# S5 mixer of a four-layer diffusion backbone: the two turned-back products are added before the output product, the outputs follow one block later, and the tables' transfers change buffers and order

## The chip, the cores and the metric

The kernel runs on one core of a Trainium2 chip. The metric is the device time of one execution in microseconds, the median of several runs. TensorE (PE), VectorE (DVE), ScalarE (ACT) and GpSimd (POOL) work beside each other, each in the order of its own instruction queue; SyncE's queue (SP) issues most of the transfers, and GpSimd's queue the rest.

## The reference

Four layers run over 256 latent tokens and 256 context tokens of width 1024. Layer 1 mixes tokens with a bidirectional diagonal state-space layer (S5) and a gated output; the other layers pool or attend, and each layer ends with a gated ConvFFN.

```
for direction in range(2):                       # forwards, and backwards in time
    a_bar, b_bar = discretise(a_re, a_im, log_dt, b_re, b_im)
    h_ctx = scan(a_bar, einsum('blgc,gpc->blgp', u_ctx, b_bar), reverse)
    h0 = h_ctx[:, 0] if reverse else h_ctx[:, -1]     # the context's last state enters the latent scan
    bu = einsum('blgc,gpc->blgp', u_lat, b_bar); bu[entry] += a_bar * h0
    h_lat = scan(a_bar, bu, reverse)
    y += real(einsum('blgp,gcp->blgc', h, c))
g = gelu(y + d_skip * u)
out = (g @ w1 + b1) * sigmoid(g @ w2 + b2)
```

There are 64 groups of 16 channels, each with 64 complex states.

## The kernel before, in words

The mixer (`s5_mixer`) handles the 64 groups in 8 blocks of 8 groups, both token streams at once. Eight tokens form a chunk, so that a scan runs over chunks only; what happens inside a chunk is held in tables. Four kinds of tables are computed during the FFN of layer 0 (`s5_tables`), written to DRAM, and loaded again, 1 MB each: `b` (per block: tokens to states), `c` (per block: states to tokens), `k` (per two blocks: token to token inside a chunk), `r` (per two blocks: cosines and sines by which states are turned, so that the scan has real decay factors).

One block m takes these steps:

- `finish_u` (L1473 and after): two operations that finish the normalised input tile U, on VectorE for blocks 0 and 1, on GpSimd for the others;
- `v_mm`: TensorE multiplies U by `b` into two PSUM tiles v, one per direction;
- `turned` and `decay`: ScalarE writes the sines with both signs into a part of the tile `us` (`signs`, two sets, used in turn) and the decay factors into `rtab`;
- `scan`: VectorE turns v (two products and a sum per direction: L1521, L1524, L1526) and scans it into the tile g (L1528). Then the states are turned back: GpSimd forms y1 = g times cosine (L1532) and y2 = g with real and imaginary part exchanged times sine (L1533). In block 7 y2 is formed on VectorE;
- `z_mm`: TensorE adds into the PSUM tile z the products of U with `k` (16 records of this kind in the trace per block) and of y1 and then of y2 with `c` (64 records each), and ScalarE applies the GELU (tile G).

`back` and `back_in` send G through DRAM, two blocks at a time, to change its layout, on GpSimd's queue; `split_hi` and `split_lo` split it into a high and a low part (gh, gl) for the GLU (`glu_mm`), whose weights come in 1 MB blocks (raw), are split by ScalarE (whi) and VectorE (wlo, L159), and are multiplied three times (hi·hi, hi·lo, lo·hi). Beside the GLU run the modulation chunks of a later step (ada): ScalarE scales, VectorE and GpSimd add up (ads, L321).

Order and buffers: every engine takes its instructions as the program writes them. The loop over m in `s5_mixer` runs scan(m), U of m + 4, signs and decay of m + 2, v of m + 2, then z of m. The table `S5HOME` says for each table load in which buffer it lands: x0 to x2 are three buffers of their own (they exist only once the tables are computed), and raw, whi, wlo and ada are the weights' buffers, two each, shared in turn. A load waits until the buffer's former content has been read. `s5_ahead` runs during the last steps of the FFN of layer 0, once per 128 channels; after every second one it writes the inputs of two blocks out (s5dU) and issues some table loads and the loads of U, in a layout by groups. The loads into x0 to x2 stand at the end of `s5_tables`. In the mixer, the table `ready` ties each further load to a step of a block. All of them go through SP's one queue.

Of the kernel before, what the change touches and what calls it, by code (L numbers as in the profile page):

```python
# [9 lines left out]
F32 = mybir.dt.float32  # L10
# [6 lines left out]
P = 128  # L17
# [15 lines left out]
S5HOME = dict(t.split(":") for t in (  # L33
    "r0:x0 k0:x1 b1:x2 b0:ada c0:ada b2:whi c1:wlo b3:whi c2:wlo r2:raw k2:raw b4:ada b5:whi c3:ada r4:x0 b6:whi "
    "c4:wlo k4:x1 b7:ada c5:wlo k6:x2 r6:raw c6:ada c7:wlo").split())
GLU = ((0, 0), (1, 0), (0, 1), (1, 1), (2, 0), (2, 1), (3, 0), (3, 1))
# [8 lines left out]
class Net:  # L45
# [1209 lines left out]
    def s5_tables(self):  # L1255
# [147 lines left out]
    def s5_ahead(self, d):  # L1403
# [31 lines left out]
        self.s5_loads(("U4", "U6") if d == 7 else todo)  # L1435

# [4 lines left out]
    def s5_mixer(self, l):  # L1441
# [70 lines left out]
        def scan(m):  # L1512
# [17 lines left out]

            y1, y2 = (y[:, 1:1025].rearrange("p (d c n) -> p d c n", d=2, c=2) for y in ys[m % 2])
            nc.gpsimd.tensor_mul(y1, g, cs)  # L1532
            (V if m == KD - 1 else nc.gpsimd).tensor_mul(y2, g[:, :, ::-1], sn[:, :, ::-1])  # L1533

        G = {}

        def z_mm(m):
            ct, kt = (self.s5tab.pop((x, m)) for x in "ck")
            u = U[m]
            if m % 4 == 0:  # L1540
                G[m // 4] = (pg.tile([P, 2, 8, 2, 64], F32, tag="g8", name="G1", bufs=2) if m else
                             self.up_.tile([P, 2, 8, 2, 64], F32, tag="u8", name="G0", bufs=self.u_bufs))
            pss = [self.psa.tile([P, 4, 64], F32, tag="acc", name=f"z{m}_{g2}") for g2 in range(2)]
            half = [slice(64 * i, 64 * i + 64) for i in range(2)]
            for j in range(4):
                for g2 in range(2):
                    self.mm(pss[g2][:, j], kt[:, 2 * j + g2], u[:, 2 * j + g2], j == 0, False)
            for i in range(2):
                for j in range(4):
                    for dr in range(2):  # L1550
                        for c in range(2):
                            x = ((2 * dr + c) * 4 + j) * 64
                            for g2 in range(2):
                                hv = ys[m % 2][i][half[g2], x:x + 64]
                                self.mm(pss[g2][:, j], ct[half[g2], dr, c, j], hv if dr == 0 else rev(hv),
                                        False, (i, j, dr, c) == (1, 3, 1, 1))
            for g2 in range(2):
                self.act(G[m // 4][:, m // 2 % 2, g2::2, m % 2], pss[g2], AF.Gelu_apprx_tanh)
# [59 lines left out]
        def glu_out(d):  # L1618
# [10 lines left out]
            if d == 0:  # L1629
                self.sq_start(LC)  # L1630
            self.sq(d)

        ready = {("v", 0): ("b4",), ("v", 2): ("b5",), ("v", 3): ("b6",), ("v", 4): ("b7",),
                 ("s", 1): ("r4",), ("s", 3): ("r6",), ("z", 0): ("c3",), ("z", 1): ("c4", "k4"),
                 ("z", 2): ("c5", "k6"), ("z", 3): ("c6",), ("z", 4): ("c7",)}

        def step(x, m, fn):
            fn(m)
            self.s5_loads(ready.get((x, m), ()))
# [3 lines left out]
        decay(1)  # L1643
        turned(1)
        for m in range(2):
            finish_u(m, V)
            finish_u(m + 2, nc.gpsimd)
            step("v", m, v_mm)
        for m in range(KD - 1):
            step("s", m, scan)  # L1650
            finish_u(m + 4, nc.gpsimd)
            turned(m + 2)
            decay(m + 2)
            step("v", m + 2, v_mm)
# [505 lines left out]
```

## Time and profile before

| | |
|---|---|
| median of 3 runs | 1798.7 us (1798.41 to 1803.33) |
| profiled execution | 1799.21 us, its span 1797.4 us |
| busy share of the span | TensorE 93%, VectorE 73%, ScalarE 45%, GpSimd 26% |
| granted TensorE clock, mean of the span | 0.964 of full speed |
| DMA, mean over the span | 199 GB/s |
| the mixer's place in the span | first v at 524.0 us, last z ends at 639.5 us, GLU until 744.7 us |

The span is the profiler's stretch from the first to the last instruction; the execution's own time lies 1.8 us above it. A timeline row gives the start, the length and the engine of one instruction or of several equal ones that follow each other (x and their number); in brackets stands how long the engine had been idle before it and who ended that. A product in float32 that is not rounded (v and z) leaves two records. `SPq` and `POOLq` are the queues' own issue instructions.

### The profile page before, as it was taken

The page shows a single profiled execution, that of the slowest core. Times are in us where ns is not written, and L with a number is a line of the kernel's source. Part 1 is how long each engine was busy: PE and PEld are TensorE (multiplying, and loading weights), DVE is VectorE, ACT ScalarE, POOL GpSimd, SP SyncE. Part 2 cuts the span into 40 slices and gives each one's busy share as a digit, 9 for nine tenths or more (in the row PEclk, how much of TensorE's full clock was granted, in tenths as well). Part 3 has the DMA queues.
Part 4 walks back from the last instruction along what each step waited for, and adds up shares of the span by engine and source line. Part 5 has one row for each costly group of instructions (what it writes and reads, how often), then busy time and mean ns, then how long its engine had stood idle before and what let it go on. Part 6 is the DMA issues. An engine that isn't in the chain of part 4 may idle for free.

```text
span 1797.4 us, 27444 instructions
## 1 busy us (share of the span) xinstructions
PE 1670.0 (93%) x10866; PEld 1385.2 (77%) x10866; DVE 1320.4 (73%) x1979; ACT 816.9 (45%) x1256; POOL 467.7 (26%) x343
## 2 busy tenths in 40 slices
PE   7889999999959996899999989999999889999998
PEld 4468777787748985687887867787678889989997
DVE  6768878888726458687887687726659888679885
ACT  4534323232333244454242543446657466466553
POOL 0015555555427427000000340201222413002000
PEclk9999999999978998999999999999999899989999
DMA  9668997768676653344546655333326656645553
GB/s 381 262 208 227 309 323 225 212 203 256 175 269 259 234 213 117 118 141 146 225 160 212 220 213 182 117 112 106 109 95 253 236 188 207 226 147 167 187 192 112
DMA packets 98184, 356.92 MB, mean 199 GB/s; under 512 B 14296, under 2 KB 37368, under 8 KB 72200
## 3 DMA queue, kind: packets, MB, share of 16 engines
q1 hardware_dynamic: 93400, 334.09, 55.0%
q0 software_dynamic: 4656, 21.08, 3.3%
q8 instruction: 86, 1.41, 0.3%
q14 instruction: 42, 0.34, 0.1%
HBM read 324.19 MB, written 30.94 MB: 198 GB/s over the span
## 4 chain that ended last, share of the span: by engine, by line
PE 63%; DVE 15%; DMA 5%; ACT 4%; issue 4%; POOL 1%; SPq 1%; ACTq 0%; DVEq 0%; POOLq 0%
PE p L61 28%; PE dn L61 16%; DVE wlo L159 6%; PE z L61 4%; PE v L61 3%; DVE t L55 2%; PE k L61 2%; DMA s5fl<-s5dA 2%; PE glu L61 2%; PE wo L61 1%; ACT whi L58 1%; PE q L61 1%; PE adp L61 1%; DMA raw<-in_wup_dram 1%; PE o L61 1%
## 5 line engine op out<-in xcount | busy, mean ns | idle before, releaser
L159 DVE TENSOR_TENSOR wlo<-raw,whi 128x1024 fp32r<-128x1024 f32 x334 | 424.3, 1312 | 124.8 <-ACT whi L58 123.6
L61 PE MATMUL p<-uh,whi 128*128 128x512 f32 (+1 forms) x1408 | 485.9, 345 | 27.0 <-DVE t L55 18.4
L61 PE MATMUL p<-uh,wlo 128*128 128x512 f32 (+1 forms) x1408 | 481.1, 342 | 4.9 <-DVE wlo L159 2.7
L61 PE MATMUL p<-ul,whi 128*128 128x512 f32 (+1 forms) x1408 | 481.5, 342 | 0.4 <-DVE ul L55 0.4
L58 ACT ACTIVATE whi<-raw 128x1024 fp32r<-128x1024 f32 x352 | 318.2, 952 | 242.9 <-PE dn L61 68.9
L61 PEld LDWEIGHTS p<-uh,whi 128*128 128x128 f32 x1408 | 272.1, 193 | 70.3 <-issue 17.5
L61 PEld LDWEIGHTS p<-uh,wlo 128*128 128x128 f32 x1408 | 271.9, 193 | 36.8 <-DVE wlo L159 4.4
L61 PEld LDWEIGHTS p<-ul,whi 128*128 128x128 f32 x1408 | 272.2, 193 | 31.9 <-DVE ul L55 2.8
L61 PE MATMUL dn<-ah,wlo 128*128 128x512 f32 (+1 forms) x704 | 240.6, 342 | 7.9 <-DVE wlo L159 7.9
L61 PE MATMUL dn<-ah,whi 128*128 128x512 f32 (+1 forms) x704 | 241.9, 344 | 5.5 <-ACT whi L58 2.9
L61 PE MATMUL dn<-al,whi 128*128 128x512 f32 (+1 forms) x704 | 239.8, 341 | 6.2 <-DVE al L819 6.2
L55 DVE SCALAR_TENSOR_TENSOR t<-p,conv_sb,t 128x510 f32<-128x510 f32 (+1 forms) x352 | 208.1, 612 | 30.8 <-ACT t L58 24.5
L321 POOL TENSOR_TENSOR ads<-ads,ada 128x2048 f32<-128x2048 f32 (+1 forms) x24 | 95.4, 3983 | 402.8 <-ACT ada L58 392.0
L61 PEld LDWEIGHTS dn<-ah,whi 128*128 128x128 f32 x704 | 135.5, 192 | 29.4 <-issue 9.6
L61 PEld LDWEIGHTS dn<-ah,wlo 128*128 128x128 f32 x704 | 135.4, 192 | 24.8 <-DVE wlo L159 10.3
L61 PEld LDWEIGHTS dn<-al,whi 128*128 128x128 f32 x704 | 135.2, 192 | 21.0 <-DVE al L819 6.7
L58 ACT ACTIVATE t<-p,conv_sb 128x512 f32<-128x512 f32 (+1 forms) x176 | 107.6, 661 | 53.9 <-PE p L61 53.8
L58 ACT ACTIVATE ah<-t 128x512 fp32r<-128x512 f32 (+1 forms) x88 | 46.0, 523 | 146.9 <-DVE t L810 137.1
L55 DVE SCALAR_TENSOR_TENSOR h<-dn,mods,h 128x256 f32<-128x256 f32 x192 | 83.8, 476 | 38.7 <-PE dn L61 38.5
L58 ACT ACTIVATE t<-t 128x512 f32<-128x512 f32 (+1 forms) x88 | 45.9, 522 | 145.4 <-DVE t L55 136.6
L55 DVE SCALAR_TENSOR_TENSOR ads<-ada,cT_sb,ads 128x2048 f32<-128x2048 f32 (+1 forms) x49 | 104.2, 2147 | 6.1 <-DMA ada<-in_ada_dram 5.2
L1316 POOL TENSOR_TENSOR s5ct<-s5bc,s5pw 128x512 f32<-128x512 f32 x32 | 41.7, 1304 | 216.5 <-DMA s5bc<-in_s5c_dram 157.2
(258 smaller groups left out, 2405.0 us busy)
## 6 DMA issues: line engine op xcount, KB each, us to landing
raw<-in_wup_dram SPq DMA_DIRECT2D x88, 1024.0 KB, 5.1
ada<-in_ada_dram SPq DMA_DIRECT2D x84, 1024.0 KB, 7.7
raw<-in_wdn_dram SPq DMA_DIRECT2D x32, 768.0 KB, 4.7
raw<-in_wdn_dram SPq DMA_DIRECT2D x32, 640.0 KB, 4.0
raw<-in_qkv_dram SPq DMA_DIRECT2D x12, 1024.0 KB, 4.9
ada<-in_ada_dram POOLq DMA_DIRECT2D x12, 1024.0 KB, 5.4
s5bt<-in_s5bT_dram SPq DMA_DIRECT2D x32, 256.0 KB, 7.1
s5fl<-s5dA SPq DMA_DIRECT2D x32, 256.0 KB, 7.6
```

The lines of the kernel that those rows point to most:

```text
L55: return self.nc.vector.scalar_tensor_tensor(out, in0, scalar, in1, op0=op0, op1=op1, **kw)
L58: return self.nc.scalar.activation(out, in_, func, **kw)
L61: return self.nc.tensor.matmul(out, lhsT, rhs, start=start, stop=stop)
L159: self.nc.vector.tensor_sub(lo[:, s], t[:, s], hi[:, s].bitcast(F32))
L321: self.nc.gpsimd.tensor_add(y, y, t)
L1316: G.tensor_tensor(ct[:, o], *x, op=ALU.mult)
```

## The change

Four things change together.

The sum: y1 and y2 are added before the output product (`join`, L1535 of the changed kernel), on VectorE for blocks 0 to 3 and 7 and on GpSimd for blocks 4 to 6, so that `z_mm` multiplies one tile by `c` instead of two.

The U products of `z_mm`: each 128x128 product with `k` is written as two products of 64 output columns each.

The order: z of block m - 1 now follows scan and v of blocks m and m + 2; the sum of block m - 1 stands behind scan(m) on VectorE; z of block 7 stands ahead of the whole first GLU weight block, and low parts of blocks 0 and 1 of G are formed on VectorE instead of GpSimd.

The transfers: `S5HOME` gives the tables other buffers; r0, k0 and b1 are loaded where r2, k2 and b2 were, and r2, b3 and k2 go into x0 to x2; the write of the last inputs (s5dU7) stands ahead of b2 and c2; the last load of U stands behind the loads of x0 to x2. In `ready`, b5 and b6 follow v of blocks 1 and 2 (before 2 and 3), and k6 follows z of block 3 (before 2).

```diff
-    "r0:x0 k0:x1 b1:x2 b0:ada c0:ada b2:whi c1:wlo b3:whi c2:wlo r2:raw k2:raw b4:ada b5:whi c3:ada r4:x0 b6:whi "
+    "r0:raw k0:raw b0:ada c0:ada b1:whi c1:wlo b2:whi c2:wlo r2:x0 k2:x1 b3:x2 b4:ada b5:whi c3:ada r4:raw b6:whi "
...
-        self.s5_loads(("r0", "b1", "k0"))
+        self.s5_loads(("r2", "b3", "k2"))
...
-        todo = {1: ("r2",), 3: ("U0", "k2"), 5: ("b2", "c1", "U2"), 7: ("b3", "c2")}.get(d, ())
-        self.s5_loads(todo if d == 7 else ())
+        todo = {1: ("r0",), 3: ("U0", "k0"), 5: ("b1", "c1", "U2"), 7: ("b2", "c2", "U4")}.get(d, ())
...
-        self.s5_loads(("U4", "U6") if d == 7 else todo)
+        self.s5_loads(todo)
...
+        def join(m, eng):
+            y = ys[m % 2][0][:, 1:1025]
+            eng.tensor_add(y, y, ys[m % 2][1])
...
-                    self.mm(pss[g2][:, j], kt[:, 2 * j + g2], u[:, 2 * j + g2], j == 0, False)
-            for i in range(2):
-                for j in range(4):
-                    for dr in range(2):
...
+                    for xs in half:
+                        self.mm(pss[g2][xs, j], kt[:, 2 * j + g2, xs], u[:, 2 * j + g2], j == 0, False)
+            for j in range(4):
+                for dr in range(2):
...
+        self.s5_loads(("U6",))
...
-        for m in range(KD - 1):
+        for m in range(KD):
             step("s", m, scan)
+            if 0 < m < 5:
+                join(m - 1, V)
+            if 3 < m < KD - 1:
+                join(m, nc.gpsimd)
             finish_u(m + 4, nc.gpsimd)
...
-            if m in (2, 4, 6):
+            if m in (3, 5, 7):
                 back(m // 2 - 1)
-            if m in (4, 6):
+            if m in (5, 7):
                 back_in(m // 2 - 2)
...
-            step("z", m, z_mm)
...
+            if m:
+                step("z", m - 1, z_mm)
...
-        scan(KD - 1)
+        self.prep_lo()
+        join(KD - 1, V)
+        split_hi(0)
+        z_mm(KD - 1)
```

SP's queue, from the last inputs to the first loads of the mixer proper (s5b1 is table `b` of block 1, s5dU5 the inputs of blocks 4 and 5, U0 and U4 the tiles of blocks 0 to 3 and 4 to 7). Before:

```order
L1384 DMA s5b2_4352<-s5dB_128 128x2048
L1387 DMA s5c1_4354<-s5dC_129 128x2048
L1382 DMA U0_4227<-s5dU3_4283 128x8x128
L1384 DMA s5b3_4403<-s5dB_128 128x2048
L1387 DMA s5c2_4405<-s5dC_129 128x2048
L1431 DMA s5dU7_4407<-us4_4323 128x1024
L1382 DMA U4_4324<-s5dU5_4350 128x8x128
L1382 DMA U4_4324<-s5dU7_4407 128x8x128
L1390 DMA s5r0_4415<-s5dR_131 128x2x1024
L1384 DMA s5b1_4417<-s5dB_128 128x2048
L1394 DMA s5k0_4419<-s5dK_130 128x2x1024
L1384 DMA s5b4_4522<-s5dB_128 128x2048
```

And now:

```order
L1384 DMA s5b1_4352<-s5dB_128 128x2048
L1387 DMA s5c1_4354<-s5dC_129 128x2048
L1382 DMA U0_4227<-s5dU3_4283 128x8x128
L1430 DMA s5dU7_4403<-us4_4323 128x1024
L1384 DMA s5b2_4405<-s5dB_128 128x2048
L1387 DMA s5c2_4407<-s5dC_129 128x2048
L1382 DMA U4_4324<-s5dU5_4350 128x8x128
L1390 DMA s5r2_4414<-s5dR_131 128x2x1024
L1384 DMA s5b3_4416<-s5dB_128 128x2048
L1394 DMA s5k2_4418<-s5dK_130 128x2x1024
L1382 DMA U4_4324<-s5dU7_4403 128x8x128
L1384 DMA s5b4_4520<-s5dB_128 128x2048
```

r0 and k0 now stand further up, in the places where r2 and k2 stood before; b1 has b2's place, s5dU7 has moved ahead of two tables, and the second load of U4 behind three.

GpSimd's queue in blocks 4 and 5 (y00 and y10 are y1 of even and odd blocks, y01 and y11 y2; in the changed kernel y10280 and y10281, and y10240 and y10241; s5dG1 is G of blocks 2 and 3 written out, gt0 G of blocks 0 to 3 read back). Before:

```order
L1532 TENSOR_TENSOR y00_4432<-g_5104,s5r4_4709 128x1024
L1533 TENSOR_TENSOR y01_4433<-g_5104,us4_4323 128x1024
L1564 DMA s5dG1_4429<-G0_4617 128x1024
L1569 DMA gt0_5156<-s5dG0_4428 128x8x128
L1532 TENSOR_TENSOR y10_4436<-g_5237,s5r4_4709 128x1024
L1533 TENSOR_TENSOR y11_4437<-g_5237,us4_4323 128x1024
```

And now:

```order
L1530 TENSOR_TENSOR y10280_4431<-g_4951,s5r4_4630 128x1024
L1531 TENSOR_TENSOR y10240_4432<-g_4951,us4_4323 128x1024
L1535 TENSOR_TENSOR y10280_4431<-y10280_4431,y10240_4432 128x1024
L1530 TENSOR_TENSOR y10281_4434<-g_5060,s5r4_4630 128x1024
L1531 TENSOR_TENSOR y10241_4435<-g_5060,us4_4323 128x1024
L1535 TENSOR_TENSOR y10281_4434<-y10281_4434,y10241_4435 128x1024
L1566 DMA s5dG1_4428<-G0_4673 128x1024
L1571 DMA gt0_5113<-s5dG0_4427 128x8x128
```

A sum stands behind each pair of products, and the transfers of G stand one block later.

VectorE's queue between the scans of blocks 1 and 2 (x2 is a turned half of v, s5r2 the table `r` of blocks 2 and 3). Before:

```order
L1528 SCALAR_TENSOR_TENSOR g_4696<-rtab10_4472,v1_0_4528 128x512
L1528 SCALAR_TENSOR_TENSOR g_4696<-rtab11_4474,v1_1_4529 128x512
L1521 TENSOR_TENSOR x2_4834<-v2_0_4581,us4_4323 128x512
L1521 TENSOR_TENSOR x2_4836<-v2_1_4582,us4_4323 128x512
L1524 TENSOR_TENSOR v2_0_4581<-v2_0_4581,s5r2_4240 128x512
```

And now:

```order
L1526 SCALAR_TENSOR_TENSOR g_4617<-rtab10_4469,v1_0_4526 128x512
L1526 SCALAR_TENSOR_TENSOR g_4617<-rtab11_4471,v1_1_4527 128x512
L1535 TENSOR_TENSOR y10280_4431<-y10280_4431,y10240_4432 128x1024
L1519 TENSOR_TENSOR x2_4729<-v2_0_4581,us4_4323 128x512
L1519 TENSOR_TENSOR x2_4731<-v2_1_4582,us4_4323 128x512
L1522 TENSOR_TENSOR v2_0_4581<-v2_0_4581,s5r2_4414 128x512
```

The sum of block 0 stands behind the scan of block 1 and ahead of block 2; it waits for GpSimd's second product of block 0.

## Rows read from the trace of the kernel before

**Rows 1.** The page's head.
```profile
span 1797.4 us, 27444 instructions
```

**Rows 2.** Engines by stretch: length, busy us of each, TensorE's clock, DMA share, GB/s.
```profile
515.00:545.00 30.00, 8.64 (x131) 7.19 (x131) 9.31 (x17) 6.85 (x14) 5.49 (x13) 0.66 0.94 347
545.00:615.00 70.00, 69.92 (x1286) 68.63 (x1283) 43.74 (x60) 17.08 (x36) 44.08 (x25) 0.98 0.62 230
```

**Rows 3.** The chain that ended last, 515 to 660 us: start, length, what.
```profile
522.91 10.52 DMA s5dU<-us
...
534.04 5.83 DMA s5r<-s5dR
...
549.53 9.22 PE z L61 x144
558.75 2.02 PE v L61 x64
...
624.73 5.71 PE glu L61 x24
630.44 9.07 PE z L61 x144
...
643.09 3.80 ACT ads L58 x2
```

**Rows 4.** Timeline of the mixer's start: start, length, engine, operation, idle before.
```profile
515.18 0.38 SPq L1384 DMA_DIRECT2D s5b<-s5dB  x1
...
524.00 3.68 PE L61 MATMUL v<-U,s5b 128*64 128x64 f32 x64 [3.09 <-DVE U L1479]
...
540.26 1.15 ACT L58 ACTIVATE us<-s5r 128x512 f32<-128x512 f32 x2 [20.58 <-DMA s5r<-s5dR]
...
541.50 1.29 DVE L1521 TENSOR_TENSOR x<-v,us 128x512 f32<-128x512 f32 x2 [16.22 <-ACT us L58]
...
545.10 2.32 DVE L1528 TENSOR_TENSOR_SCAN g<-rtab,v 128x512 f32<-128x512 f32 x2
```

**Rows 5.** Timeline of one block, GpSimd and TensorE, 554 to 570 us.
```profile
554.51 2.41 POOL L1532 TENSOR_TENSOR y<-g,s5r 128x1024 f32<-128x1024 f32 x1
...
556.87 2.37 POOL L1533 TENSOR_TENSOR y<-g,us 128x1024 f32<-128x1024 f32 x1
...
560.69 2.00 PE L61 MATMUL z<-U,s5k 128*128 128x64 f32 x16
561.57 2.36 POOL L1532 TENSOR_TENSOR y<-g,s5r 128x1024 f32<-128x1024 f32 x1
...
562.62 7.36 PE L61 MATMUL z<-y,s5c 64*128 64x64 f32 x128
```

**Rows 6.** Timeline, GpSimd and VectorE, at the mixer's end and in the GLU.
```profile
616.50 0.93 POOL L1569 DMA_DIRECT2D gt<-s5dG  x1
616.59 2.36 DVE L159 TENSOR_TENSOR wlo<-raw,whi 128x1024 fp32r<-128x1024 f32 x2 [0.36 <-ACT whi L58]
...
648.91 4.65 POOL L321 TENSOR_TENSOR ads<-ads,ada_t 128x2048 f32<-128x2048 f32 x1 [4.36 <-ACT ada_t L58]
649.75 10.48 DVE L159 TENSOR_TENSOR wlo<-raw,whi 128x1024 fp32r<-128x1024 f32 x2 [5.06 <-ACT whi L58]
...
654.57 5.66 DVE L159 TENSOR_TENSOR wlo<-raw,whi 128x1024 fp32r<-128x1024 f32 x1
...
703.61 11.01 POOL L321 TENSOR_TENSOR ads<-ads,ada_t 128x2048 f32<-128x2048 f32 x2
```

**Rows 7.** DMA issues, 440 to 660 us: operation, KB each, median us to landing.
```profile
s5b<-s5dB SPq DMA_DIRECT2D x7, 1024.0 KB, 10.4
...
s5dG<-G POOLq DMA_DIRECT2D x4, 512.0 KB, 5.3
gt<-s5dG POOLq DMA_DIRECT2D x4, 512.0 KB, 7.4
```

**Rows 8.** Groups of GpSimd's instructions by shape: busy us, mean ns.
```profile
L321 POOL TENSOR_TENSOR ads<-ads,ada 128x1024 f32<-128x1024 f32 x10 | 27.7, 2790 | 75.9 <-ACT ada L58 65.4 <-issue 10.5
```

More of the change, by code (lines that the diff above doesn't have):

```diff
@@ L33 @@
 S5HOME = dict(t.split(":") for t in (
-    "r0:x0 k0:x1 b1:x2 b0:ada c0:ada b2:whi c1:wlo b3:whi c2:wlo r2:raw k2:raw b4:ada b5:whi c3:ada r4:x0 b6:whi "
-    "c4:wlo k4:x1 b7:ada c5:wlo k6:x2 r6:raw c6:ada c7:wlo").split())
+    "r0:raw k0:raw b0:ada c0:ada b1:whi c1:wlo b2:whi c2:wlo r2:x0 k2:x1 b3:x2 b4:ada b5:whi c3:ada r4:raw b6:whi "
+    "c4:wlo k4:raw b7:ada c5:wlo r6:x0 k6:x1 c6:ada c7:wlo").split())
 GLU = ((0, 0), (1, 0), (0, 1), (1, 1), (2, 0), (2, 1), (3, 0), (3, 1))
@@ L1450, in s5_mixer @@
         for i in range(2):
-            ys.append([pp.tile([P, 1028], F32, tag=f"y{i}{x}", name=f"y{i}{x}", bufs=1) for x in range(2)])
-            for t in ys[i]:
-                nc.gpsimd.memset(t[:, 0:1], 0.0)
+            ys.append([pp.tile([P, n], F32, tag=f"y{n}{i}", name=f"y{n}{i}", bufs=1) for n in (1028, 1024)])
+            nc.gpsimd.memset(ys[i][0][:, 0:1], 0.0)
         signs = [self.s5us[:, 1024 * i:1024 * i + 1024].rearrange("p (d s n) -> p d s n", d=2, s=2) for i in range(2)]
@@ L1529, in scan @@
                                      v.rearrange("p c n -> p (c n)"), 0.0, ALU.mult, ALU.add)
-            y1, y2 = (y[:, 1:1025].rearrange("p (d c n) -> p d c n", d=2, c=2) for y in ys[m % 2])
+            y1, y2 = (y.rearrange("p (d c n) -> p d c n", d=2, c=2) for y in (ys[m % 2][0][:, 1:1025], ys[m % 2][1]))
             nc.gpsimd.tensor_mul(y1, g, cs)
             (V if m == KD - 1 else nc.gpsimd).tensor_mul(y2, g[:, :, ::-1], sn[:, :, ::-1])
+        def join(m, eng):
+            y = ys[m % 2][0][:, 1:1025]
+            eng.tensor_add(y, y, ys[m % 2][1])
         G = {}
@@ L1546, in z_mm @@
                 for g2 in range(2):
-                    self.mm(pss[g2][:, j], kt[:, 2 * j + g2], u[:, 2 * j + g2], j == 0, False)
-            for i in range(2):
-                for j in range(4):
-                    for dr in range(2):
[L1551 to L1556, printed above, removed]
+                    for xs in half:
+                        self.mm(pss[g2][xs, j], kt[:, 2 * j + g2, xs], u[:, 2 * j + g2], j == 0, False)
+            for j in range(4):
+                for dr in range(2):
+                    for c in range(2):
+                        x = ((2 * dr + c) * 4 + j) * 64
+                        for g2 in range(2):
+                            hv = ys[m % 2][0][half[g2], x:x + 64]
+                            self.mm(pss[g2][:, j], ct[half[g2], dr, c, j], hv if dr == 0 else rev(hv),
+                                    False, (j, dr, c) == (3, 1, 1))
             for g2 in range(2):
@@ L1631, in glu_out @@
             self.sq(d)
-        ready = {("v", 0): ("b4",), ("v", 2): ("b5",), ("v", 3): ("b6",), ("v", 4): ("b7",),
+        ready = {("v", 0): ("b4",), ("v", 1): ("b5",), ("v", 2): ("b6",), ("v", 4): ("b7",),
                  ("s", 1): ("r4",), ("s", 3): ("r6",), ("z", 0): ("c3",), ("z", 1): ("c4", "k4"),
-                 ("z", 2): ("c5", "k6"), ("z", 3): ("c6",), ("z", 4): ("c7",)}
+                 ("z", 2): ("c5",), ("z", 3): ("c6", "k6"), ("z", 4): ("c7",)}
         def step(x, m, fn):
@@ L1656, in s5_mixer @@
                 self.prep_hi()
-            if m in (2, 4, 6):
+            if m in (3, 5, 7):
                 back(m // 2 - 1)
-            if m in (4, 6):
+            if m in (5, 7):
                 back_in(m // 2 - 2)
-            if m == 6:
-                split_hi(0)
-                split_lo(0, nc.gpsimd)
-            step("z", m, z_mm)
-            if m == 3:
+            if m:
+                step("z", m - 1, z_mm)
+            if m in (5, 6):
                 self.limit = self.n_dma + 1
                 self._fill_dma()
-        scan(KD - 1)
+        self.prep_lo()
+        join(KD - 1, V)
+        split_hi(0)
+        z_mm(KD - 1)
         self.limit = len(self.blocks)
         self._fill_dma()
+        split_lo(0)
         split_hi(1)
-        self.prep_lo()
         split_lo(1)
@@ L1678, in s5_mixer @@
         ws = self.take()
+        back(3)
         glu_mm(0, 0, ws, (0,))
-        z_mm(KD - 1)
         self.ada_ahead()
-        back(3)
         back_in(3)
```

## The prediction

> **What bounds the kernel now.** I read the page's head first: the span is 1797.4 us [rows 1]; the profiled execution as a whole took 1799.2, and the median of the runs in the table is 1798.7, half a microsecond less. Then the engines by stretch [rows 2]. The reader should see two different states of the S5 mixer there. From 515 to 545 us TensorE is busy 8.6 us of 30 while the DMA engines are busy 0.94 of the time: nothing computes and everything loads. From 545 to 615 TensorE is busy 69.9 us of 70 while VectorE is busy 43.7 and GpSimd 44.1, and the DMA engines 0.62: there TensorE is the bound. The chain of waits says the same [rows 3]. Ahead of the blocks it goes through two transfers: 10.5 us for s5dU (the last pair of blocks written out), behind which the second U4 load stands on SP's queue, and then 5.8 us for s5r, the table of blocks 0 and 1, which could only be issued at 534.0. After that it is TensorE alone, 9.22 us of z and 2.02 us of v per block, 11.24 together.
>
> The timeline of the start shows what the late table holds up [rows 4]: the first v is there from 524.0, but ScalarE waits 20.6 us for s5r, VectorE's first turn starts at 541.5, and the scan of block 0 ends at 547.4.
>
> The timeline of one block gives the prices [rows 5]. GpSimd takes 7.06 us from one y to the next (554.51 to 561.57: two turned-back products and the two finishing operations of U). TensorE takes 1.9 us for the sixteen U products (560.69 to 562.62) and 7.3 us for the 128 y products.
>
> **The change part by part.**
>
> *Start.* SP's order now has r0, k0 and b1 where r2, k2 and b2 stood, and the second U4 load stands behind r2, b3 and k2. r0 is fourteen places further ahead in that queue, in front of all four U loads, so the waits of [rows 3, 4] for s5r fall away. What is late next is v of block 0 itself: 64 records from 524.00, 3.68 us at the lower clock, until 527.7 [rows 4]. VectorE's block takes 5.9 us (541.50 to 547.42); its first operation, 0.65 us, runs while the second half of v is still coming, so the scan of block 0 ends at 527.7 + 5.3 = 533.0 instead of 547.4. b1 has the place that b2 had, issued at 515.2; with the median of 10.4 us for such a load [rows 4, 7] it is there at 525.6, in time for v of block 1. U2 stands where it was.
>
> *TensorE per block.* The y products fall from 128 to 64 records, 7.3 to 3.64 us. The sixteen U records of 128x128 weights become 32 of 128x64. That form has run here only for v: 64 records in 2.02 us, 1.0 us for 32 [rows 3]. The other end is that splitting brings nothing and each costs 0.12 us as now, 3.9 us. I take 1.0, since v's operands have the same shapes. A block is then 2.0 + 1.0 + 3.6 = 6.7 us of TensorE against 11.24. That is less than GpSimd's 7.06, so TensorE stops being the bound, and the 4.5 us per block are not all mine.
>
> *The sums.* Five on VectorE (blocks 0 to 3 and 7), three on GpSimd (4 to 6). On VectorE alone such an operation, 128x1024 from two SBUF operands, takes 1.2 us (half of the 2.36 for two) [rows 6]. It won't be alone: GpSimd is in its products nearly all the time. The rows show the same kind of VectorE operation beside a GpSimd addition: started at 649.75, its first half ended at 654.57, just behind the end of the addition that had begun at 648.91 (4.65 us), and the second took 5.66. Two GpSimd additions among such operations took 11.01 us, 0.9 more each than that 4.65 [rows 6]. So they take turns, and each VectorE sum pushes GpSimd back by about its own 1.2 us. GpSimd's y products beside the scan's operations, which read one operand from PSUM, keep their 2.36 to 2.41 us [rows 5].
>
> [...]
>
> VectorE has room: 5.9 + 1.2 is 7.1 us a block. So a round on GpSimd is 7.06 + 1.2 = 8.3 us while U is being finished, four rounds; then three rounds of two products and a sum. The sum on GpSimd isn't in the trace: it lies between 2.36 us (a product of that size, [rows 5]) and 2.79 (the mean of ten additions of that size, [rows 8]); I take 2.4, because the products are operations of this very place.
>
> *The chain from the scan of block 0 to the last sum*, on GpSimd, from 533.0:
> - four rounds of 7.06: 28.2
> - four VectorE sums let in between: 4.8
> - three rounds of 2 x 2.36 + 2.4: 21.4
> - three DMA issues (G0 and G1 out, G0 back) of at most 0.93 [rows 6]: 2.7
> - block 7: the second product on VectorE 1.2 (the sum's size), the first on GpSimd 2.4, and the two halves of the first GLU weight's wlo and the last sum, all on VectorE behind it, 3.6: together 7.2
> - some 15 hand-overs between the two engines at an estimated 0.1: 1.5
>
> That makes 65.8, so the last sum ends at 598.8 (and the first, which releases z0, a round after 533.0, at about 541.4). The other chains are shorter: ScalarE's signs for block m + 2 wait for the second product of block m, which ends a scan earlier; TensorE needs 6.7 of the 8.3 us.
>
> *End.* z of block 7 has its U part done and needs 3.6: 602.4. The first GLU weight block, 2 x 5.7 us [rows 3], now stands whole behind z7, where its first half stood ahead of it. Its third step needs G of blocks 2 and 3 back: that load is issued behind the last y product at 596.9, takes 7.4 us [rows 7], and 1.3 more for hi and lo: 605.6, where TensorE would come at 605.2. So 602.4 + 11.4 + 0.4 = 614.2. Before, z7 ended at 639.5 and the same block at 639.5 + 5.7 = 645.2 [rows 3]. The gain is 31.0 us.
>
> *Behind it* the GLU's weights and modulation chunks are the same work in the same sequence. The chain of waits runs there over ScalarE, which scales the first chunk (ads) at 643.1 [rows 3], behind hi of blocks 4 and 5. Those come back later relative to z7 than now: G out at 596.2, 5.3 us, and back, 7.4 [rows 7], so 608.9, and ads 1.2 later at 610.1, which is 33.0 earlier than before. That chain thus moves forward by 2 us more than TensorE does, and I count nothing for it; the third weight block, 22.8 us of TensorE behind z7, is the first to need what hangs on it.
>
> **Sum:** 1799.2 - 31.0 = 1768.2 us, and against the median of the runs half a microsecond less. I say 1768. Its own bounds: the U split at 3.9 us makes TensorE the bound from z0 at 541.4 (8 x 7.5 + 4 x 2.0 = 68, so 609.5 instead of 602.4), 1775; the lock partly missed, 1764.
>
> **The rivals.**
>
> *The two engines don't get in each other's way.* VectorE's sum could slip into the moments when GpSimd waits. Then the four sums, the product and one half of wlo cost GpSimd nothing, 6 x 1.2 = 7.2 us: 1761. Against it speak the rows of the blocked operations [rows 6]; for it, that GpSimd's additions there last twice as long as its operations here. Chance 0.12.
>
> *The tables become the bound.* Behind 515.2 there are 20 loads of 1.05 MB and four of 0.52, 23.1 MB, until c7. They must be in by 598.8, which is 276 GB/s. The start ran at 347, the blocks at 230 [rows 2]. At 347 they are done by 582. At 230 the last lands at 615.6, 16.8 later: 1785. For it: each load waits for a buffer that a block frees, in one queue, so a late one holds all behind it. Against it: 230 was all that the slower blocks asked for. Between the ends, 1777. Chance 0.16.
>
> *TensorE's clock stays low.* Before the blocks the granted clock is 0.66 on the mean, and 0.98 once TensorE runs without a break [rows 2]. Now it would have a gap in every block. [...] Against it: at the low level a block is 13.3 us of TensorE in a round of 8.3, which leaves no gap, and without gaps the clock stood at 0.98 [rows 2]. Chance 0.08. [...]
>
> **How the numbers follow.** My own case has 0.64 (1764 to 1776), the rivals 0.12, 0.16 and 0.08. The range 1759 to 1784 takes in the first two and most of the third; it leaves out the fourth and the upper end of the third. A measurement of this kernel tells about 0.3% from no change, 5.4 us. All cases but the last are faster by more: 0.92; of the last I give 0.05 to slower and 0.03 to within.
>
> **What would show it.** Right: no wait of ScalarE for s5r; the first turn near 526; z of 96 records per block with waits for the sums between; VectorE's sums of 1.2 us and up to 3.6 where GpSimd is inside an operation, and GpSimd operations of 3.5 us behind them; about 8.3 us from block to block at first and 7.1 later; the first GLU product near 602. Wrong: TensorE without gaps from v to v (the U split brings nothing or the clock is low), or waits of v, of z or of ScalarE's signs for s5b, s5c or s5r (the tables), or a GLU stage longer than before.

## The result, and the profile after

| | before | changed kernel |
|---|---|---|
| median us (range, runs) | 1798.56 (1795.33 to 1803.33, 4) | 1773.95 (1771.89 to 1777.81, 4) |
| profiled execution, us | 1799.21 | 1773.63 |
| first v, first GLU product, last GLU product, us | 524.0, 624.7 (half a weight block ahead of z7), 744.7 | 521.1, 610.6, 721.3 |

The ratio is 0.9864, 95% interval [0.9836, 0.9891]: faster by 1.4%, 24.6 us of the medians. Forecast were 1768 us and a range of 1759 to 1784. In the profiled executions 25.6 us went: 2.9 before the first v, 20.5 between the first v and the last GLU product, 2.2 behind it. Nothing shows the 2.9 or the 2.2 to be the change's: in the fourteen profiled executions of this study the first v lies anywhere from 520.3 to 526.0, and from the last GLU product to the end of the span it is anywhere from 1045.2 to 1053.8 us, with the kernels in no order.

The page's head of the changed kernel, to be held against [rows 1]:

```profile
span 1771.8 us, 26687 instructions
```

Engines by stretch (length; busy us of PE, PEld, DVE, ACT, POOL; TensorE's clock; DMA share; GB/s), to be held against [rows 2]:

```profile
515.00:545.00 30.00, 15.87 (x328) 15.43 (x328) 25.80 (x35) 9.43 (x18) 19.34 (x14) 0.77 1.00 378
545.00:600.00 55.00, 45.46 (x862) 44.16 (x860) 39.69 (x47) 15.63 (x32) 44.45 (x24) 0.82 0.85 323
600.00:614.50 14.50, 14.03 (x118) 12.80 (x116) 3.70 (x5) 5.28 (x10) 0.99 (x2) 0.51 0.37 134
```

The loading stretch now also computes. In the blocks a round of TensorE now takes 6.67 us (from v to v, 546.95 to 553.62) and one of GpSimd 7.86 (530.26 to 538.12), as meant; but TensorE starts late, for a table, and stays behind its sums (both below). The surprise is the last line: TensorE is busy 14.0 of 14.5 us, at half the clock.

The start on the timeline (start, length, engine, operation; in brackets the idle time before and who ended it), to be held against [rows 4]:

```profile
521.09 5.98 PE L61 MATMUL v<-U,s5b 128*64 128x64 f32 x128 [3.09 <-DVE U L1477]
...
523.21 0.69 DVE L1519 TENSOR_TENSOR x<-v,us 128x512 f32<-128x512 f32 x1 [0.85 <-PE v L61]
...
527.82 2.32 DVE L1526 TENSOR_TENSOR_SCAN g<-rtab,v 128x512 f32<-128x512 f32 x2
...
538.34 3.69 PE L61 MATMUL v<-U,s5b 128*64 128x64 f32 x64 [6.90 <-DMA s5b<-s5dB]
```

VectorE's wait of 16.2 us, behind s5r, is gone; the scan of block 0 ends 9 us behind the start of the first v. Table `b` of block 3 is late instead (that of block 2 too, by 2.27 us). VectorE takes up v of block 3 only at 545.05, when it has been there for 3 us. But z of block 0 stands behind that v on TensorE: it begins at 541.77, 4.5 us behind its sum (537.25).

The blocks, on GpSimd and VectorE, to be held against [rows 5]:

```profile
526.89 1.06 POOL L1477 TENSOR_TENSOR U<-U,s5sh 128x512 f32<-128x512 f32 x1
...
547.14 2.40 POOL L1530 TENSOR_TENSOR y<-g,s5r 128x1024 f32<-128x1024 f32 x1 [1.09 <-PE z L61]
...
551.87 2.28 DVE L1535 TENSOR_TENSOR y<-y,y 128x1024 f32<-128x1024 f32 x1 [0.91 <-POOL y L1531]
...
553.14 1.93 POOL L1477 TENSOR_TENSOR U<-U,s5sh 128x512 f32<-128x512 f32 x1
...
584.09 3.20 POOL L1535 TENSOR_TENSOR y<-y,y 128x1024 f32<-128x1024 f32 x1
...
593.14 1.22 DVE L1535 TENSOR_TENSOR y<-y,y 128x1024 f32<-128x1024 f32 x1
```

A VectorE sum beside GpSimd takes up to 2.28 us instead of 1.22, and GpSimd's short U operation 1.93 instead of 1.06: each holds the other up. In e11 below, where no sum of blocks 0 to 3 runs on VectorE, all six of these U operations take 1.06.

In what follows, raw38 is the first GLU weight block as loaded, whi38 and wlo38 are its high and low part, c7 is table `c` of block 7, and z5 is z of block 5. The end, on TensorE, ScalarE and SP's queue:

```profile
578.61 0.66 ACT L58 ACTIVATE G<-z 128x256 f32<-128x256 f32 x2 [0.97 <-PE z L61]
589.77 2.00 ACT L58 ACTIVATE whi<-raw 128x1024 fp32r<-128x1024 f32 x2 [10.50 <-DMA raw<-in_glu_dram]
591.68 0.64 ACT L58 ACTIVATE G<-z 128x256 f32<-128x256 f32 x2
...
578.65 0.32 SPq L1387 DMA_DIRECT2D s5c<-s5dC  x1
579.07 14.51 SPq L129 DMA_DIRECT2D raw<-in_glu_dram  x3
...
580.29 3.79 PE L61 MATMUL z<-y,s5c 64*128 64x64 f32 x64
592.10 2.03 PE L61 MATMUL z<-U,s5k 128*64 128x64 f32 x32 [8.02 <-ACT G L58]
594.06 7.09 PE L61 MATMUL z<-y,s5c 64*128 64x64 f32 x64
...
610.61 0.79 PE L61 MATMUL glu<-gh,whi 128*128 128x512 f32 x1
```

Read it from the bottom. The GLU waits for z7, and z7 and z6 take 9.1 us each, where z5 took 5.0. TensorE stood still for 8.0 us ahead of z6, for the GELU of z5, which frees z6's PSUM bank. That GELU stands on ScalarE behind whi38, which waits for raw38's transfer, issued only at 579.07, behind z4 and c7. This order is the change's own, by a hunk that the diff ahead of the prediction does not show:

```diff
-            if m == 3:
+            if m in (5, 6):
                 self.limit = self.n_dma + 1
                 self._fill_dma()
```

In the kernel before, raw38 was issued behind z3, 11 us ahead of c7, and whi38 did not wait for it. SP's rows there:

```profile
592.90 0.42 SPq L129 DMA_DIRECT2D raw<-in_glu_dram  x1
603.75 0.32 SPq L1387 DMA_DIRECT2D s5c<-s5dC  x1
```

The chain of waits has the same steps, and it goes back beyond them to the late table of block 3, over TensorE alone:

```profile
527.18 11.02 DMA s5b<-s5dB
...
538.34 3.69 PE v L61 x64
542.02 5.00 PE z L61 x96
...
565.51 1.05 issue
566.56 4.10 PE z L61 x35
570.66 3.27 PE v L61 x64
573.93 4.70 PE z L61 x96
...
579.07 10.62 DMA raw<-in_glu_dram
589.77 2.00 ACT whi L58 x2
592.10 9.11 PE z L61 x96
601.62 9.06 PE z L61 x96
```

From 538.3 to z4's end at 578.6 TensorE stands still once, for 1.05 us. No z waits for its sum; the y products of z4 begin 4.2 us behind theirs (570.6), and raw38 is issued behind them. The clock fell there too: it was 0.51 from 566.5 to 573.0, where 35 z records took 4.10 us and v of block 6 took 3.27 instead of 2.02, and 1.00 again from 573.5.

### The profile page after: what moved, and what is told of

Same layout as the page of the kernel before. It is cut to its first block, busy times and chain, and to the rows that moved or that the text cites. A ratio compares the mean times of both kernels' runs of the same rounds, so it can differ in the third digit from the quotient of the medians.

```text
span 1771.8 us, 26687 instructions
## 1 busy us (share of the span) xinstructions
PE 1648.2 (93%) x10482; PEld 1362.7 (77%) x10482; DVE 1329.9 (75%) x1986; ACT 817.1 (46%) x1256; POOL 478.1 (27%) x342
## 4 chain that ended last, share of the span: by engine, by line
PE 64%; DVE 14%; DMA 6%; ACT 4%; issue 4%; SPq 1%; POOL 1%; DVEq 0%; ACTq 0%; POOLq 0%
PE p L61 31%; PE dn L61 14%; DVE wlo L159 6%; PE v L61 3%; PE z L61 3%; DVE t L55 2%; PE k L61 2%; DMA raw<-in_wup_dram 2%; DMA s5fl<-s5dA 2%; PE glu L61 2%; PE wo L61 1%; ACT whi L58 1%; PE q L61 1%; PE adp L61 1%; PE o L61 1%
## 5 line engine op out<-in xcount | busy, mean ns | idle before, releaser
L61 PEld LDWEIGHTS dn<-ah,whi 128*128 128x128 f32 x704 | 135.0, 192 | 28.4 <-issue 8.7
L1316 POOL TENSOR_TENSOR s5ct<-s5bc,s5pw 128x512 f32<-128x512 f32 x32 | 45.4, 1418 | 219.5 <-DMA s5bc<-in_s5c_dram 154.3
```

What stands on the lines that cost most here:

```text
L61: return self.nc.tensor.matmul(out, lhsT, rhs, start=start, stop=stop)
L1316: G.tensor_tensor(ct[:, o], *x, op=ALU.mult)
```

## The experiments

Two theories for the lost end. **A**: whi38 ahead of the GELU of z5 opens the gap, and the low clock is nothing but the gap's consequence; without the wait both go. **B**: the low clock is a cause of its own. B was sharpened from run to run; each expectation has it as it stood then. Times below are medians; each run was timed beside the kernel before on the same chip (1796.9 to 1798.7 us). "First v", "first GLU" and "last GLU" are starts in the profiled execution.

| run | median us | ratio to before, 95% | first v | first GLU | last GLU |
|---|---|---|---|---|---|
| changed kernel | 1773.95 | 0.9864 [0.9836, 0.9891] | 521.1 | 610.6 | 721.3 |
| e1 | 1769.98 | 0.9835 [0.9802, 0.9868] | 520.9 | 605.4 | 716.2 |
| e2 | 1770.2 | 0.9845 [0.9819, 0.987] | 524.9 | 606.1 | 716.8 |
| e3 | 1788.54 | 0.994 [0.9911, 0.9969] | 523.5 | ahead of z7 | 737.1 |
| e4 | 1787.41 | 0.9942 [0.9919, 0.9964] | 524.5 | 621.7 | 735.3 |
| e5 | 1768.04 | 0.9841 [0.9817, 0.9864] | 521.9 | 604.9 | 715.6 |
| e6 | 1774.06 | 0.988 [0.9859, 0.99] | 526.0 | 612.0 | 722.9 |
| e7 | 1774.38 | 0.9882 [0.986, 0.9904] | 522.0 | 611.2 | 722.0 |
| e8 | 1776.94 | 0.9889 [0.9868, 0.991] | 523.5 | 615.8 | 726.6 |
| e9 | 1768.96 | 0.9836 [0.9814, 0.9857] | 521.2 | 606.5 | 718.7 |
| e10 | 1768.75 | 0.9837 [0.9815, 0.9859] | 520.9 | 602.7 | 713.3 |
| e11 | 1778.41 | 0.9888 [0.9869, 0.9906] | 524.7 | 619.0 | 729.7 |
| e12 | 1765.66 | 0.9826 [0.9809, 0.9842] | 520.3 | 601.0 | 713.3 |

The intervals of e1, e2, e5, e9, e10 and e12 overlap each other, and all of them that of the changed kernel. So the times rank these runs poorly; what the argument rests on is the rows.

**e1: whi38 behind z5 on ScalarE.**

```diff
-            if m == 6:
-                self.prep_hi()
...
             if m:
                 step("z", m - 1, z_mm)
+            if m == 6:
+                self.prep_hi()
```

> The split of the first GLU weight by ScalarE (whi38) is moved behind z and G of block 5; nothing else changes. Theory A (the loss at the end is this split: it waits 10.5 us for its weight, G5 stands behind it, z6 waits 8.0 us for G5's bank, and the gap brings the low clock): G5 is done near 585, z6 runs from about 587.4 behind the sum of block 6, z7 ends between 598 and 602 instead of 610.6, and the time falls by 9 to 12 us, to 1762 to 1765. Theory B (the gaps between the sums bring the low clock at the end anyway, and the last sum sets the end): z7 ends within 2 us of 610.6 and the time stays at 1772 to 1776.

1770.0, 4 us less: neither A's 9 to 12 nor B's none. whi38 held nothing up any more, but TensorE waited 2.05 us ahead of z5 for the GELU of z4, which stands on ScalarE behind the signs of block 7, and from there to the GLU the clock stood at 0.50. TensorE's rows, and the stretch:

```profile
577.38 2.04 PE L61 MATMUL z<-U,s5k 128*64 128x64 f32 x32 [2.05 <-ACT G L58]
579.35 7.09 PE L61 MATMUL z<-y,s5c 64*128 64x64 f32 x64
```

```profile
577.00:605.40 28.40, 27.08 (x288) 26.27 (x288) 12.99 (x13) 4.85 (x11) 13.39 (x9) 0.50 0.78 294
```

TensorE is busy 27.1 of 28.4 us with z alone, and the clock does not come back. That speaks against A.

**e2: the transfer of that weight block issued ahead of c7.**

```diff
+            if m == 5:
+                self.limit = self.n_dma + 1
+                self._fill_dma()
             if m:
                 step("z", m - 1, z_mm)
-            if m in (5, 6):
+            if m == 6:
```

> whi38 stays where it is, but its weight raw38 is issued ahead of the last table c7 instead of behind it. Theory A (the weight was late because it stood in SP's queue behind c7, which waits for z4): raw38 is issued near 573.5 instead of 579.1, lands near 583, ScalarE waits for it 3 to 5 us instead of 10.5, z6 follows its sum, and the time falls by 8 to 12 us, to 1762 to 1766. Theory B (low clock in any case): 1772 to 1776. If c7 then comes late instead, z7 waits for s5c and the gain is below 4 us.

1770.2, again between the two ranges: the wait for raw38 is gone as well, by the other way, and the clock fell all the same, in a wait of 1.47 us for a sum:

```profile
589.91 6.72 PE L61 MATMUL z<-y,s5c 64*128 64x64 f32 x64 [1.47 <-POOL y L1535]
```

**e3 and e4: the two halves of the change apart.** e3 is the kernel before with the hunks on `S5HOME`, `s5_ahead` and `ready` and the new loads, e4 the changed kernel without them.

One line of each, e3 against before and e4 against the changed kernel:

```diff
-        self.s5_loads(("r0", "b1", "k0"))
+        self.s5_loads(("r2", "b3", "k2"))
```

```diff
-        self.s5_loads(("r2", "b3", "k2"))
+        self.s5_loads(("r0", "b1", "k0"))
```

> The kernel before with the change's homes, places and order of the tables' transfers alone; two products per block as before. Theory A (the late s5r cost the start, and the blocks after it are TensorE's 11.24 us each): the first turn moves from 541.5 to about 526, the blocks stay at 11.2 us, and the time falls by 13 to 16 us, to 1783 to 1786. Theory B (the tables are late in either order, so another table is waited for): less than 6 us.

> The changed kernel with the homes and order of the tables' transfers of the kernel before. Theory A: the start is the old one (first turn near 541), then about 8 us per block; the last sum comes near 612, the time falls by 12 to 20 us, to 1779 to 1787. Theory B (the sums were only fast because the tables came in the new order): blocks of 10 us or more with waits for s5b, s5c or s5r, and less than 8 us of gain.

Each half alone gives 0.6% (10.8 and 10.4 us by the ratios), together 1.4%, 24.5 us: they add, within the intervals. Both came out above the range expected of theory A, e3 by 2.5 us (its ten runs lie from 1778.8 to 1803.0) and e4 by 0.4. With the transfers alone the first v leads straight into blocks of 11.2 us of TensorE, as before; but in e3 the clock fell in z6, whose y products took 13.59 us where they took 7.36 before. With the sums alone ScalarE waits for s5r as before, and the end runs at the low clock as in the changed kernel (its mean over the span is 0.950, lower than the changed kernel's 0.957). ScalarE's row of e4:

```profile
540.10 1.15 ACT L58 ACTIVATE us<-s5r 128x512 f32<-128x512 f32 x2 [19.93 <-DMA s5r<-s5dR]
```

**e5: z5 and z7 in the PSUM banks of v6 and v7**, so that no GELU holds z5, z6 or z7; nothing is reordered.

```diff
-            pss = [self.psa.tile([P, 4, 64], F32, tag="acc", name=f"z{m}_{g2}") for g2 in range(2)]
+            zp = (self.psu, "up") if m in (5, 7) else (self.psa, "acc")
+            pss = [zp[0].tile([P, 4, 64], F32, tag=zp[1], name=f"z{m}_{g2}") for g2 in range(2)]
```

> The changed kernel with z5 and z7 in two other PSUM banks (those of v6 and v7), so that no z after z4 waits for the GELU of the block before; nothing is reordered, raw38 and whi38 stay where they are. Both theories: the 8.0 us wait of TensorE before z6 goes, and z6 waits for its sum (about 587.3) instead. Theory B (the low clock is a matter of its own: it falls in any gap of 2 us or so, and the 64-row products do not raise it again): z6 and z7 still run at 0.50 with 2.0 and 7.1 us, the first GLU product comes at about 604 to 606 instead of 610.6, and the time is 1767 to 1770. Theory A (the low clock came from the 8 us gap alone): the clock holds, z7 ends about 0.2 + 3.8 us behind the last sum (594.4), the GLU starts at 598 to 599 and the time is 1761 to 1763.

1768.0: Theory B's number. z6 no longer waits for a GELU but for its sum, and from that wait on the clock is low:

```profile
583.59 1.15 PE L61 MATMUL z<-U,s5k 128*64 128x64 f32 x32
588.92 7.09 PE L61 MATMUL z<-y,s5c 64*128 64x64 f32 x64 [4.18 <-POOL y L1535]
...
597.85 7.09 PE L61 MATMUL z<-y,s5c 64*128 64x64 f32 x64
```

**e6: e5 with extra products in the gaps**, behind z4, z5 and z6, whose result nobody reads.

```diff
+            n = {4: 16, 5: 32, 6: 32}.get(m, 0)
+            if n:
+                ps = self.psm.tile([P, 512], F32, tag="misc0", name=f"hold{m}")
+                u7 = self.s5u[7][1]
+                for i in range(n):
+                    i %= 8
+                    self.mm(ps[:, :64], u7[:, 128 * i:128 * i + 128], U[7][:, i], True, True)
```

> As the run before, with products of 128 x 128 weights by 64 columns into a spare PSUM bank, whose result nobody reads: 16 behind z4, 32 behind z5, 32 behind z6 (about 1, 2 and 2 us at the full clock, which is the time that TensorE has over there). Theory B: with the gaps filled the granted clock stays at 1.00, z6 and z7 take 1.1 and 3.8 us, the GLU starts at 598 to 600, 5 to 7 us before the run without them, and the time is 1762 to 1765. Rival (filling does not matter, z products alone let the clock fall): clock 0.50 all the same, the extra products take twice as long and stand in the way, the GLU starts at 608 or later, and the time is no better than the changed kernel's 1774.

Theory B's clock with the rival's time. The clock held, 1.00 over the whole stretch, and the y products of z6 and z7 took 3.79. But the 0.06 us at which I had priced an extra product was an estimate that no row had shown, and they take 0.23 (7.36 us for 32), so they stood in the way of z6 and z7, and the time is no better than the changed kernel's. TensorE's rows, and the stretch:

```profile
587.85 7.36 PE L61 MATMUL hold<-U 128*128 128x64 f32 x64
595.14 1.15 PE L61 MATMUL z<-U,s5k 128*64 128x64 f32 x32
596.22 3.79 PE L61 MATMUL z<-y,s5c 64*128 64x64 f32 x64
```

```profile
575.00:612.00 37.00, 37.00 (x536) 36.28 (x532) 20.25 (x19) 6.95 (x14) 20.39 (x11) 1.00 0.70 265
```

**e7: e6 with whi38 behind z5**, as in e1.

> As the run before, with whi38 also behind z5 on ScalarE. It tells whether what the GLU needs (whi38, wlo38, the first halves) becomes the bound once z ends early. If TensorE's last z is all that holds the GLU: same as the run before within 1 us (1762 to 1765). If GELU of z5 and z6 behind whi38 delay the blocks' way through DRAM: 1 to 3 us less than the run before.

1774.4, the same as e6, with the clock at 1.00 as well: with the extra products filling TensorE and z5 and z7 in other banks, the order on ScalarE costs nothing.

**e8: the changed kernel with undivided U products.**

```diff
-                    for xs in half:
-                        self.mm(pss[g2][xs, j], kt[:, 2 * j + g2, xs], u[:, 2 * j + g2], j == 0, False)
+                    self.mm(pss[g2][:, j], kt[:, 2 * j + g2], u[:, 2 * j + g2], j == 0, False)
```

> The changed kernel with the 16 U products of a block undivided (128 x 128 weights, as before the change). Theory of the prediction (the dividing costs nothing, 1.1 against 1.0 us at the full clock): within 0.1% of the changed kernel, z6 and z7 at 0.50 as there. Rival (the undivided products hold or raise the clock): granted clock above 0.6 between 592 and 610, first GLU product before 607, time 1768 to 1771.

Neither expectation holds: 1776.9, 3 us above the changed kernel by the medians (the intervals overlap), and from the first v to the first GLU product 92.3 us instead of 89.5. The clock is as low as there, and the dividing is worth something by itself: 2.00 us undivided against 1.10 at the full clock, 3.67 against 2.03 at the low one, of which the last two blocks pay the second.

```profile
552.14 2.00 PE L61 MATMUL z<-U,s5k 128*128 128x64 f32 x16
...
594.02 3.67 PE L61 MATMUL z<-U,s5k 128*128 128x64 f32 x16 [6.95 <-ACT G L58]
```

**e9 and e10: e5 with the sum of block 7 ahead of wlo38 on VectorE**; e9 with 14 extra products behind z5 besides.

```diff
-        self.prep_lo()
         join(KD - 1, V)
+        self.prep_lo()
```

> z5 and z7 in other banks as in the run e5, the sum of block 7 on VectorE ahead of wlo38 (it had stood behind it, and so behind whi38 and raw38: 593.3 instead of 591.2 in e5), and 14 of the extra products behind z5 alone: 14 x 0.23 = 3.3 us, which is the 4.2 us that TensorE waits there for the sum of block 6. The extra products are sized this time by their measured price (0.23 us each, where I had put 0.06). Theory B (a gap lowers the clock, z does not raise it, other work in the gap holds it): clock 1.00 to the GLU, z6 and z7 with 1.1 and 3.8 us, first GLU product at 597 to 599 instead of 604.9 in e5, time 1760 to 1763. Rival (the GLU waits for something else by then: wlo38, the first halves, the transfers through DRAM): TensorE waits before or in the first GLU block, first product at 601 or later or gaps behind it, time 1764 to 1768.

> As e9 without the extra products. Theory B: clock 0.50 from the gap before z6 on, z6 and z7 y products 7.1 us each, first GLU product at 603.5 to 605 (the earlier sum of block 7 is worth nothing, since z7 stands behind z6), time 1766 to 1769, as e5. Rival (the clock is no matter): the same time as e9.

The same time, 1768.96 and 1768.75; e10's number was expected, e9's not. In both the clock fell already during z5, after two waits that I had left uncovered (0.82 and 0.92 us in e9). The extra products came too late, took 0.22 us a record instead of 0.12, and did not raise it either. e9's rows:

```profile
577.71 4.80 PE L61 MATMUL z<-y,s5c 64*128 64x64 f32 x64 [0.92 <-POOL y L1535]
582.45 6.23 PE L61 MATMUL hold<-U 128*128 128x64 f32 x28
...
590.52 7.09 PE L61 MATMUL z<-y,s5c 64*128 64x64 f32 x64
```

**e11: the sums of blocks 0 to 3 on GpSimd too.**

```diff
-            if 0 < m < 5:
-                join(m - 1, V)
-            if 3 < m < KD - 1:
+            if m < KD - 1:
                 join(m, nc.gpsimd)
```

> The changed kernel with the sums of blocks 0 to 3 on GpSimd as well (as 4 to 6), one block earlier each. The sums on VectorE held GpSimd up by about 0.9 us each, a sum on GpSimd takes it 2.36 us. [...] Rival 1 of the prediction (the engines do not get in each other's way): 4 x 2.36 = 9.4 us, time 1782 or more. Rival (GpSimd has slack in these rounds): 1773 to 1775.

1778.4, below the range of Rival 1 and above that of the other. By the two figures at the head of the expectation, four sums are 4 x (2.36 - 0.9) = 5.8 us more for GpSimd; the rows show 6.0. From y1 of block 0 to y1 of block 7 it is 61.9 us, in the changed kernel 57.0, and 1.09 of these are the wait for a z that e11 does not have. That makes the 6.0 us for four sums, 1.5 each, that is, a sum of 2.36 on GpSimd less the 0.87 that a VectorE sum had cost it. The groups of that line, changed kernel and e11:

```profile
L1530 POOL TENSOR_TENSOR y<-g,s5r x8: 2335/2374/2400, 530.3 to 587.3; 128x1024 f32<-128x1024 f32 x8
```

```profile
L1530 POOL TENSOR_TENSOR y<-g,s5r x8: 2338/2372/2400, 533.8 to 595.7; 128x1024 f32<-128x1024 f32 x8
```

**e12: e10 with extra products where it waited**: 3 ahead of z4, 5 and 14 between the U and the y products of z5 and z6.

```diff
+            if m == 4:
+                hold(3)
             for j in range(4):
...
+            if m in (5, 6):
+                hold({5: 5, 6: 14}[m])
             for j in range(4):
```

> The run e10 (z5 and z7 in other banks, sum of block 7 ahead of wlo38) with extra products just where TensorE waited there, at 0.23 us each: 3 ahead of z4 (it waited 0.60 us), 5 between the U and the y products of z5 (0.94 us), 14 between those of z6 (2.64 us, and what z6 comes earlier). Theory B (the clock falls in a wait that no work covers, and neither z nor extra products raise it afterwards, but while it is up, work in the waits holds it): clock 1.00 from 555 to the GLU, z5 to z7 y products 3.8 us each, z7 ends at 595.5 to 597, first GLU product there instead of 602.7, time 1761 to 1764. Rival (the fall around 580 in e9 and e10 has another cause than the waits): clock 0.50 from 580 on, extra products 0.22 us a record there, first GLU product at 606 or later, time 1768 to 1772.

1765.7, the lowest median, between the range of Theory B and the rival's. The clock held to z6 and fell within its y products, behind the one wait that was left (1.05 us, since the sum came later than the 14 products lasted); so only z7 ran slow. TensorE's rows:

```profile
582.88 3.34 PE L61 MATMUL hold<-U 128*128 128x64 f32 x28
587.26 4.87 PE L61 MATMUL z<-y,s5c 64*128 64x64 f32 x64 [1.05 <-POOL y L1535]
...
593.96 7.09 PE L61 MATMUL z<-y,s5c 64*128 64x64 f32 x64
600.99 0.79 PE L61 MATMUL glu<-gh,whi 128*128 128x512 f32 x1
```

The GLU starts 1.7 us earlier than in e10 and ends at the same 713.3. At 687.3 it is still 1.6 us ahead; then, behind a wait of 2.67 us for wlo, the clock falls and is 0.50 from 689.0 to 692.0. In e10, behind 1.88 us at the same place, it did not fall.

What the twelve runs settle: A is right for the 8 us gap (e1, e2 and e5 each remove it), and wrong for the clock, which was low at the end of each of them. B is right in this much: the fall does not need whi38's wait, and over the full stretches of e6 and e7, where TensorE had no gap, and in e12 up to its last gap, the clock stayed at 1.00.

What lets it fall is not settled. It fell in or behind uncovered waits of 0.8 to 8.0 us, but waits of 0.94 (e6), 0.98 (e11), 1.17 and 1.32 us (e4) passed without a fall. It also fell in e3, where 0.47 us was all the wait that showed, while the kernel before stood the same 0.47 us ahead of its z6 without a fall.

What the engine did when it rose, the rows show. Inside the blocks it rose each time during a v or at most 1.5 us behind one: in the changed kernel at 573.2, and likewise in e2, e4, e5, e7 and e11. In e11 9.1 us of z alone, from 569.4, left it low, and behind the v that followed it was 1.00 from 583.5. Behind the last v it was low in eleven kernels, all but the kernel before, e6 and e7; there no z raised it, and it came back in the GLU. So a fall in the middle lasted until the next v, and one behind the last v until the GLU.

## Why the prediction was right, and where its sum was off

The time is 6 us above the forecast and within the likeliest case's bounds, but not all by that case: parts of the second and third rival took place too. Some of the agreement may be luck: of the 25.6 us of the profiled executions 5.1 lie ahead of the first v and behind the GLU, where the kernels scatter by more than that. Between the two the gain was 20.5 us. By its steps:

- **Start.** The scan of block 0 was to end at 533.0; it ended at 530.1, and the mixer began 2.9 us earlier, so from the start of the first v it is 9.0 us, as forecast. Right, and e4, where ScalarE still waits 19.9 us for s5r, shows that the transfers bring it.
- **TensorE per block.** Forecast 6.7 us; the chain of waits has 4.65 to 5.0 of z and 2.02 of v. The U split was to bring z's U part to 1.0; it is 1.10. Right; e8 prices the split at 0.9 us a block. The waits for sums that the prediction named as a sign did not come: TensorE was late, by the table of block 3 first and then by the wait and the low clock around 566 to 573.
- **The sums.** Each VectorE sum was to push GpSimd back by 1.2 us. The direction is right, the size was less: the U operations beside them show 0.87 (1.93 against 1.06), and e11 gives the same. The first rival, two engines that don't get in each other's way, falls with the same rows, 2.28 us instead of 1.22 on the one side and 1.93 instead of 1.06 on the other. The prediction bounds its sum by a lock that is partly missed (1764); no run shows a lock as such, only that the operations last longer beside each other, by up to 1.06 us on VectorE and 0.87 on GpSimd.
- **Chain to the last sum.** Forecast 65.8 us; from 530.1 to 594.4 it took 64.2. The sum is right to 1.6 us, its parts less so: up to the end of GpSimd's last product it was 59.4 us where the terms make 62.2, and from there to the last sum 4.8 instead of 3.6, because that sum stands on VectorE behind wlo38, which waits 5.76 us for whi38, and so for the same transfer.
- **"z of block 7 has its U part done and needs 3.6: 602.4."** This step failed. From the last sum to the first GLU product it took 16.3 us. The claim ahead of it, "The other chains are shorter", put whi38 at nothing without a reason: its transfer, ahead of c7 before, now stands behind z4 and c7, and whi38 itself stands ahead of the GELU of z5. That is a gap of 8.0 us, and then two z at the low clock, 9.1 instead of 4.9 each. The first GLU weight block ended at 623.4, 9.2 us later than forecast: 4.4 better by start and chain (2.9 of it the earlier first v), 12.7 worse here, 0.9 worse in the block itself, whose first products still ran low.
- **"at the low level a block is 13.3 us of TensorE in a round of 8.3, which leaves no gap, and without gaps the clock stood at 0.98"** This argument, by which I discounted the third rival, assumed that TensorE without gaps gets its clock back. In the middle of the blocks the clock did come back: it was low for 6.5 us (0.51 from 566.5 to 573.0) and rose with a v. Behind the last v it did not: it was 0.50 from 592.0 to 610.6 with TensorE shown busy for 18.0 of the 18.6 us. The low clock cost some 3.3 us of TensorE's time in the middle (4.10 us for 35 z records and 3.27 for a v) and some 9 us in z6, z7 and the first GLU products. An estimate from these rows for all eight z and four v at the low level, 9.1 and 3.69 us each instead of 4.9 and 2.02, is some 40 us more; what the low clock cost is under a third of that. e1 shows the low level standing for 28.4 us with TensorE shown busy for 27.1. The rows agree that the clock falls around waits and that filled waits hold it (1.00 in e6), but TensorE shown busy did not raise it: behind z products (e1) and behind the extra products (e9) it stayed low, and it came back in the GLU (in the changed kernel 0.67 from 610.6 to 616.3 and 1.00 from there to 623.4).
- **The tables as the bound.** Half true: the DMA engines are busy all of 515 to 545 us (a share of 1.00), v2 waits 2.27 and v3 6.9 us for their tables. On GpSimd's path that is at most the 1.09 us it waited for a z at 547.1. On TensorE's it is more: the chain that ended last goes from this table over z0 to z4, and raw38 is issued behind z4. How much of the late end this makes stays open; no run varied it alone.
- **Behind it, nothing.** The first GLU block ended 21.8 us earlier than before, the whole execution 25.6. Of the difference 1.6 came back within the GLU and 2.2 behind it. Counting nothing was a little too low here; the 2.2 are less than the scatter there, and in e12 a lead of 1.7 us was lost within the GLU.

So the gain of 31.0 us was 21.8 at the place where it was summed, and the 5.4 us that the profiled execution missed are the end's 12.7 less 4.4 and less the 3.8 that came behind, plus 0.9 in the GLU's first block.

## What to carry to other kernels

When a step is moved a block later, look at what every in-order engine now has ahead of it there: here one weight conversion, waiting for a transfer at the end of a queue, held a GELU, and with it a PSUM bank and TensorE. Price the end of a pipeline at both clock levels, 1.00 and 0.50 here: a short wait there can cost twice, by itself and by the clock (z6 and z7 took 9.1 us each instead of 4.9). The conversion behind z5 (e1), its transfer further ahead (e2) and banks of their own for the last tiles (e5) brought the GLU's first product forward by 4.5 to 5.7 us each. Filling the waits as well brought it forward by another 1.7 (e12 against e10), and nothing of that was left at the GLU's end. Price filler work from a row before placing it.

## What was not expected of the hardware

- A granted clock that had fallen to 0.50 stayed there while TensorE was shown busy 27.1 of 28.4 us with z products (e1), and through 6.2 us of extra products (e9); the same extra products in the waits kept a clock that was up at 1.00 (e6, e7). Where a v still followed, it came back each time, during the v or at most 1.5 us behind it (3.27 us of v in the changed kernel).
- The U part of a block takes 1.10 us as 16 products into 64 output columns, and 2.00 us as 8 into 128 (e8): a factor of 1.8 for products that were whole before.
